# Row gathers begun during the routing stage, query weights' low parts on another engine, packed activations and a deeper ring of weight tiles

## The chip, the cores and the metric

The kernel runs on one core of one Trainium2 chip. The metric is the device time of one execution in microseconds, the median of three runs. Engines are named as in the profile: PE is TensorE, PEld its weight loads, DVE is VectorE, ACT is ScalarE, POOL is GpSimd, SP is SyncE, which here only issues DMAs.

## The reference, cut to what matters

One layer of a streaming encoder on 512 frames of width 2048: two token mixers (an RWKV7 recurrence and a sparse attention), a residual sum, then a PEER feed-forward block and a last RMS norm. The change touches the PEER block alone:

```python
q = (h @ w_query).reshape(B, T, 8, 2, 128)
s = jnp.einsum('bthcq,hcnq->bthcn', q, sub_keys)      # 128 keys a side
s1, i1 = lax.top_k(s[..., 0, :], 16)
s2, i2 = lax.top_k(s[..., 1, :], 16)
cand, cand_id = s1[..., :, None] + s2[..., None, :], i1[..., :, None] * 128 + i2[..., None, :]
top_s, pos = lax.top_k(cand.reshape(..., 256), 16)
eid, gate = take(cand_id, pos), softmax(top_s)
act = gelu(einsum('nd,nhkd->nhk', hx, expert_u[eid]))   # 16384 experts
y = einsum('nhk,nhkd->nd', gate * act, expert_v[eid])
```

Every token has 8 heads x 16 chosen experts, that is 128 rows of `expert_u` and 128 rows of `expert_v`.

## The kernel before

Weights are fp32 in HBM. To multiply them with nearly fp32 precision in the fast fp32r format, each 128x1024 weight tile (`raw`, 512 KB, loaded by SP's queue) is split: ACT copies its rounded high part (`whi`, line 198), DVE subtracts to get the low part (`wlo`, line 199), and PE does three matmuls for each product (high x high, high x low, low x high). `load_w` does this; the pool `wp` holds three `raw`, two `whi` and two `wlo`. `load_w` runs at a raised priority, so that weights are placed ahead of other work.

The order of each engine's queue is not the order of the program: a planner (the tile framework) orders the instructions by priority and by the times of a model, places buffers, and puts in the waits. Each engine then works through its own queue in order. `issue_after(x)` keeps the DVE instructions of a block behind instruction x.

The PEER block splits the tokens. The first 176 tokens are computed by gathering: for each chosen expert a row of 8 KB is fetched for each of 128 partitions by an indirect DMA from POOL (line 1005, 1 MB each, 176 from `ru` and 176 from `rv`), into three buffers (`rows`); DVE makes a dot product (line 1015) or adds a scaled row (line 1023). They come in three groups, of 16 tokens (16 items each way), 32 tokens (32) and 128 tokens (128); with the start and end of each group 364 items in all. The other 336 tokens (`ND`) are computed densely: all 16384 experts on PE, weighted by a matrix G that is zero where an expert was not chosen. This part has the following stages:

- `route`: for 8 heads x 2 sides a gemm of the query weights (512 tokens), scores, and the top-16 search on DVE (`top16`); per head four pieces of "early" dense experts (24 of 128 column groups are computed early, to use PE; their weights come through an own pool `we`). The expert numbers of the 128-token group, `eid[-1]`, are written head by head.
- G, still in `route`: for each token a one-hot product builds the columns of G, with POOL, ACT and DVE making the one-hots (`oa`, `ob`) and PE multiplying; G goes to HBM (`d_g`), and the remaining early pieces run between.
- `experts`: 16 column groups; in each, 8 activations (`act`, 336 columns, 48 matmuls each, lines 214 to 216), `gated` by G (line 1210) and split into `Wh`, `Wl`; then 16 blocks of output features with 24 matmuls each (lines 1229 to 1231), added into `accT` (line 1236). G is loaded for each column group by POOL's queue into one buffer (line 1200). Between, `step` takes up gather items at a fixed rate, each behind the last `wlo` of `load_w`.

The normalized activations of all 512 tokens, split into `h2h` and `h2l`, stay in SBUF (64 KB a partition) until the last activation; their space is then used for the final buffers (`fin`).

Of the kernel before, what the change touches and what calls it, by code (L numbers as in the profile page):

```python
# [167 lines left out]
class Kernel:  # L168
    def __init__(self, tc, io, out, dbg=None):
        self.tc, self.nc, self.io, self.out, self.dbg = tc, tc.nc, io, out, dbg or {}  # L170
        self.fins = ExitStack()
        self.blocks = ((0, 128), (1, 128), (2, ND - 256))
# [16 lines left out]
    def load_w(self, src, wp=None):  # L189

        nc = self.nc
        wp = wp or self.wp
        with self.tc.high_priority(offset=100):
            raw = wp.tile([128, 1024], F32, tag="raw", name="raw", bufs=3)
            nc.sync.dma_start(raw, src.rearrange("p a b -> p (a b)"))
            hi = wp.tile([128, 1024], F32R, tag="whi", name="whi")
            lo = wp.tile([128, 1024], F32R, tag="wlo", name="wlo")
            nc.scalar.activation(hi, raw, AF.Copy)  # L198
            self.last = nc.vector.tensor_tensor(lo, raw, hi.bitcast(F32), op=ALU.subtract).ins  # L199
        return hi, lo  # L200
# [736 lines left out]
    def peer(self):  # L937
# [3 lines left out]
        with ExitStack() as es:  # L941
# [38 lines left out]
            self.hs = lambda k: (hh[:, k, NG:T], hl[:, k, NG:T])  # L980
            with ExitStack() as es2:
                self.route(es2, lambda k: (hh[:, k], hl[:, k]))
            self.dp = R(self.pool("dense", side="right"))
# [4 lines left out]
    def step(self, items, n=1):  # L988

        self.due += n * self.rate  # L990
        while self.due >= 1:
            self.due -= 1
            with self.tc.issue_after(self.last):
                next(items, None)

    def gathered(self):
# [11 lines left out]
        for i, (t0, m, parts) in enumerate(GROUPS):  # L1008
            eid, act, n = self.eid[i], self.act_[i], 128 // parts
# [3 lines left out]
            for s in range(n):  # L1013
                r = rows(io["ru"], eid, s)
                v.tensor_tensor_reduce(r, r, h, 1.0, 0.0, op0=ALU.mult, op1=ALU.add, accum_out=act[:, s:s + 1])  # L1015
                yield
            sc.activation(act, act, AF.Gelu)
            v.tensor_tensor(act, act, self.gate[i], op=ALU.mult)
            o = row("out")
            for s in range(n):  # L1020
                r = rows(io["rv"], eid, s)
# [23 lines left out]
            yield  # L1045

# [10 lines left out]
    def route(self, es, xs):  # L1057
# [12 lines left out]
        with ExitStack() as es3:  # L1070
            tp = es3.enter_context(self.pool("top", 2))
            ts = tp.tile([128, 4, 8, 16], F32, name="ts", bufs=1)
            sel = [tp.tile([128, 4, 8, 16], F32, name=f"sel{i}", bufs=1) for i in range(2)]
            for h in range(8):
                sv = tp.tile([128, 2, 4, 16], F32, name="sv")
                si = tp.tile([128, 2, 4, 16], U32, name="si")
                sf = tp.tile([128, 2, 4, 16], F32, name="sf")
# [45 lines left out]
                for e, b in ((self.eid[-1], 0), (eid1, 1)):  # L1123
                    m = e.shape[0]
                    v.scalar_tensor_tensor(e[:, 16 * h:16 * h + 16], sel[0][:m, b, h], 128.0, sel[1][:m, b, h], op0=ALU.mult, op1=ALU.add)

# [23 lines left out]
        for tg in range(ND // 16):  # L1150
            Gs = gp.tile([128, 128, 16], F32, name="Gs")
            for b in range(4):
                i = 4 * tg + b
                n = 4 * len(EARLY) - 32
                for _ in range((i + 1) * n // (ND // 4) - i * n // (ND // 4)):
                    next(early, None)
                pg = self.wk()
# [31 lines left out]
    def experts(self):  # L1189
# [3 lines left out]
        items = self.gathered()  # L1193
        self.due = 0
        self.rate = sum(2 * (128 // g[2]) + 4 for g in GROUPS) / (256 + 2 * (128 - len(EARLY)) - 20)
        ng = ND // 16
        for cg in range(16):
# [3 lines left out]
            W = []  # L1201
            for j in range(8):
# [6 lines left out]
                a3 = a.rearrange("p (g t) -> p g t", g=ng)  # L1209
                v.tensor_tensor(a3, a3, G[:, :, j], op=ALU.mult)  # L1210
                wh = dp.tile([128, ND], F32R, name="Wh", bufs=8)
                wl = dp.tile([128, ND], F32R, name="Wl", bufs=8)
                self.split(a, wh, wl)
                W.append((wh, wl))
                if e not in EARLY:
                    self.step(items, 2)
            turn = iter(())
            if last:
                for _ in items:
                    pass  # L1220
                self.left.close()
                turn = self.turned()
            for db in range(16):
# [14 lines left out]
                self.step(items)  # L1238
# [4 lines left out]
    def turned(self):  # L1243
# [3 lines left out]
        self.fp = self.fins.enter_context(self.pool("fin"))  # L1247
# [52 lines left out]
```

## Time and profile before

| | |
|---|---|
| runs, us | 4098.62, 4097.76, 4099.79; median 4098.62 |
| profiled execution, us | 4096.14 |
| its span, us | 4094.4 |
| mean granted clock of PE | 0.985 |
| busy share PE, DVE, ACT, POOL | 95%, 70%, 34%, 23% |
| DMA moved | 946 MB, 231 GB/s over the span |

The span is what the trace covers; the execution's own time is 1.7 us longer. Matmuls overlap in the array, so PE can be busy without being at its peak; counts of matmuls in a stretch tell more than its busy share. A wait is put down to the releaser that came last.

### The profile page before, as it was taken

What the parts mean: (1) busy time and instruction counts of PE and PEld (TensorE: products, weight loads), DVE (VectorE), ACT (ScalarE), POOL (GpSimd) and SP (SyncE); (2) the same over time, 40 slices, a digit from 0 to 9 for tenths busy, and PEclk for the clock granted to TensorE, in tenths of its full rate; (3) what the DMA queues carried; (4) which work ended last, traced back from release to release, by engine and by line L of the source; (5) the groups of instructions that cost most, each with busy time, mean ns of one, the idle gap of its engine ahead of it and who ended that gap; (6) DMA issues with size and microseconds to landing.
All of it is one profiled execution on the core that took longest, in us unless ns stands there. A gap on an engine that the chain in (4) does not pass through costs nothing. (4 is left out here: it accounts for less than half of the span.)

```text
span 4094.4 us, 57543 instructions
## 1 busy us (share of the span) xinstructions
PE 3903.1 (95%) x22241; PEld 3511.4 (86%) x22241; DVE 2861.5 (70%) x4766; ACT 1393.1 (34%) x2044; POOL 958.7 (23%) x980
## 2 busy tenths in 40 slices
PE   8999999999998999999998999999999999999998
PEld 6777778888886788788898899999999999899998
DVE  5445588444434552489876778889888888889885
ACT  4222332222224422332486333333333233333333
POOL 2101210101104300100363323323332233333220
PEclk9999999999999999999999999999999999999999
DMA  4333842332327433443576989989999999999994
GB/s 150 125 125 132 198 165 83 103 101 84 99 86 199 143 131 137 144 134 107 185 220 184 346 309 368 373 310 367 360 368 369 361 370 353 353 363 367 348 352 168
DMA packets 258290, 946.17 MB, mean 231 GB/s; under 512 B 28224, under 2 KB 77504, under 8 KB 209280
## 3 DMA queue, kind: packets, MB, share of 16 engines
q1 hardware_dynamic: 132528, 445.76, 31.9%
q0 software_dynamic: 82144, 474.71, 31.3%
q10 hardware_dynamic: 43344, 22.02, 1.9%
q8 instruction: 175, 2.87, 0.3%
q14 instruction: 99, 0.81, 0.1%
HBM read 866.18 MB, written 76.12 MB: 230 GB/s over the span
## 5 line engine op out<-in xcount | busy, mean ns | idle before, releaser
L198 ACT ACTIVATE whi<-raw 128x1024 fp32r<-128x1024 f32 x758 | 802.8, 1060 | 1953.6 <-PE mm L215 871.1
L199 DVE TENSOR_TENSOR wlo<-raw,whi 128x1024 fp32r<-128x1024 f32 x758 | 927.2, 1225 | 708.3 <-ACT whi L198 645.5
L1231 PE MATMUL wk<-Wh,wlo 128*128 128x336 f32 x2048 | 658.6, 323 | 57.2 <-DVE wlo L199 57.0
L1229 PE MATMUL wk<-Wh,whi 128*128 128x336 f32 x2048 | 660.4, 323 | 16.1 <-ACT whi L198 10.9
L1230 PE MATMUL wk<-Wl,whi 128*128 128x336 f32 x2048 | 657.1, 321 | 2.3 <-DVE Wl L228 2.2
L214 PE MATMUL mm<-h2h,whi 128*128 128x336 f32 (+1 forms) x1920 | 630.6, 328 | 12.8 <-ACT gel L1181 10.9
L216 PE MATMUL mm<-h2h,wlo 128*128 128x336 f32 (+1 forms) x1920 | 630.8, 329 | 8.5 <-DVE wlo L199 8.2
L215 PE MATMUL mm<-h2l,whi 128*128 128x336 f32 (+1 forms) x1920 | 629.6, 328 | 0.0
L214 PE MATMUL mm<-xh,whi 128*128 128x512 f32 x1168 | 473.3, 405 | 2.1 <-ACT xh L346 1.5
L216 PE MATMUL mm<-xh,wlo 128*128 128x512 f32 x1168 | 468.2, 401 | 6.0 <-DVE wlo L199 6.0
L215 PE MATMUL mm<-xl,whi 128*128 128x512 f32 x1168 | 470.2, 403 | 0.6 <-POOL xl L348 0.5
L1231 PEld LDWEIGHTS wk<-Wh,wlo 128*128 128x128 f32 x2048 | 391.4, 191 | 73.5 <-DVE wlo L199 71.3
L1015 DVE CUSTOM_DVE_ANT_0 rows<-rows,h2t 128x2048 f32<-128x2048 f32 x176 | 401.7, 2284 | 44.6 <-DMA rows<-in_ru_dram,eid 44.4
L1023 DVE SCALAR_TENSOR_TENSOR out<-rows,act,out 128x2048 f32<-128x2048 f32 x173 | 405.7, 2345 | 20.8 <-DMA rows<-in_rv_dram,eid 20.0
L1229 PEld LDWEIGHTS wk<-Wh,whi 128*128 128x128 f32 x2048 | 392.2, 192 | 26.2 <-ACT whi L198 16.8
L1005 POOL DMA_INDIRECT rows<-in_ru_dram,eid x176 | 263.9, 1500 | 595.2 <-DVE act L1015 540.7
L1005 POOL DMA_INDIRECT rows<-in_rv_dram,eid x176 | 258.8, 1470 | 600.1 <-DVE out L1023 531.2
L1230 PEld LDWEIGHTS wk<-Wl,whi 128*128 128x128 f32 x2048 | 392.1, 191 | 4.3 <-DVE Wl L228 3.9
L216 PEld LDWEIGHTS mm<-h2h,wlo 128*128 128x128 f32 x1920 | 363.6, 189 | 25.6 <-DVE wlo L199 15.1
L214 PEld LDWEIGHTS mm<-h2h,whi 128*128 128x128 f32 x1920 | 363.6, 189 | 24.1 <-ACT gel L1181 11.4
L215 PEld LDWEIGHTS mm<-h2l,whi 128*128 128x128 f32 x1920 | 363.7, 189 | 10.0 <-issue 0.2
L216 PEld LDWEIGHTS mm<-xh,wlo 128*128 128x128 f32 x1168 | 221.6, 190 | 60.3 <-DVE wlo L199 6.9
(432 smaller groups left out, 5711.4 us busy)
## 6 DMA issues: line engine op xcount, KB each, us to landing
raw<-in_pu_dram SPq DMA_DIRECT2D x256, 512.0 KB
raw<-in_pv_dram SPq DMA_DIRECT2D x256, 512.0 KB
raw<-in_w_in_dram SPq DMA_DIRECT2D x146, 512.0 KB
d_g<-Gs ACTq DMA_DIRECT2D x21, 1024.0 KB
G<-d_g POOLq DMA_DIRECT2D x16, 1344.0 KB
raw<-in_wbr_dram SPq DMA_DIRECT2D x32, 512.0 KB
raw<-in_wout_dram SPq DMA_DIRECT2D x32, 512.0 KB
raw<-in_wpq_dram SPq DMA_DIRECT2D x32, 512.0 KB
```

Of the source, the lines that this page charges most:

```text
L198: nc.scalar.activation(hi, raw, AF.Copy)
L199: self.last = nc.vector.tensor_tensor(lo, raw, hi.bitcast(F32), op=ALU.subtract).ins
L214: nc.tensor.matmul(ps, hi[:, s], xh, start=k == 0, stop=False)
L215: nc.tensor.matmul(ps, hi[:, s], xl, start=False, stop=False)
L216: nc.tensor.matmul(ps, lo[:, s], xh, start=False, stop=k == nk - 1)
L1005: nc.gpsimd.indirect_dma_start(out=r, out_offset=None, in_=table, in_offset=bass.IndirectOffsetOnAxis(ap=eid[:, s:s + 1], axis=0))
L1015: v.tensor_tensor_reduce(r, r, h, 1.0, 0.0, op0=ALU.mult, op1=ALU.add, accum_out=act[:, s:s + 1])
L1023: v.scalar_tensor_tensor(o, r, act[:, s:s + 1], o, op0=ALU.mult, op1=ALU.add)
L1229: mmul(ps, hi[:, s], wh, start=j == 0, stop=False)
L1230: mmul(ps, hi[:, s], wl, start=False, stop=False)
L1231: mmul(ps, lo[:, s], wh, start=False, stop=j == 7)
```

## The change

Gather items begin in the route: two after each head, and one after every sixth of the 84 steps of G, 30 in all. For this the 128-token group's dot products come first, then the two small groups whole, then the rest of the 128-token group. During the heads, the low parts of the query weights are subtracted on POOL and not on DVE (those of early experts stay on DVE). The index tile `sf` is bf16 in place of fp32. At the end of the route, ACT and DVE copy the 336 dense tokens of `h2h` and `h2l` into packed tiles (43 KB a partition), and the old 64 KB are freed; the dense buffers and a new pool `wx` go there. `wx` has two `raw`, one `whi` and one `wlo`, which `load_w` uses in turn with those of `wp` in the dense stage, by the counter `nw`. In the first column group the six experts that are not early come first, and gating lags two experts behind. The final buffers use the packed tiles' space.

```diff
@@ load_w
+        pr = ps = wp
+        if self.wx and wp is self.wp:
+            pr, ps = wp if self.nw % 5 < 3 else self.wx, wp if self.nw % 3 < 2 else self.wx
+            self.nw += 1
-            raw = wp.tile([128, 1024], F32, tag="raw", name="raw", bufs=3)
+            raw = pr.tile([128, 1024], F32, tag="raw", name="raw", bufs=3 if pr is wp else 2)
-            hi = wp.tile([128, 1024], F32R, tag="whi", name="whi")
-            lo = wp.tile([128, 1024], F32R, tag="wlo", name="wlo")
+            hi = ps.tile([128, 1024], F32R, tag="whi", name="whi")
+            lo = ps.tile([128, 1024], F32R, tag="wlo", name="wlo")
-            self.last = nc.vector.tensor_tensor(lo, raw, hi.bitcast(F32), op=ALU.subtract).ins
+            if self.low is nc.vector or wp is not self.wp:
+                self.last = nc.vector.tensor_tensor(lo, raw, hi.bitcast(F32), op=ALU.subtract).ins
+            else:
+                self.low.tensor_tensor(lo, raw, hi.bitcast(F32), op=ALU.subtract)
@@ peer
+            self.items, self.nitems = self.gathered(), 0
             with ExitStack() as es2:
                 self.route(es2, lambda k: (hh[:, k], hl[:, k]))
-            self.dp = R(self.pool("dense", side="right"))
+            self.packed = ExitStack()
+            hp = self.packed.enter_context(self.pool("h2d", side="right"))
+            ph = hp.tile([128, 16, ND], F32R, name="ph")
+            pl = hp.tile([128, 16, ND], F32R, name="pl")
+            for a, b in ((0, 2), (2, 6), (6, 11), (11, 16)):
+                sc.activation(ph[:, a:b], hh[:, a:b, NG:T], AF.Copy)
+                v.tensor_copy(pl[:, a:b], hl[:, a:b, NG:T])
+            self.left.close()
+            self.hs = lambda k: (ph[:, k], pl[:, k])
+            self.wx = E(self.pool("wx", 1))
+            self.dp = E(self.pool("dense"))
@@ step
+    def item(self):
+        self.nitems += 1
+        with self.tc.issue_after(self.last):
+            next(self.items, None)
@@ gathered: up(i) and down(i) are the two halves of the old loop over groups
+        last = len(GROUPS) - 1
+        yield from up(last)
+        for i in range(last):
+            yield from up(i)
+            yield from down(i)
+        yield from down(last)
@@ route
+            self.low = nc.gpsimd
             for h in range(8):
-                sf = tp.tile([128, 2, 4, 16], F32, name="sf")
+                sf = tp.tile([128, 2, 4, 16], BF16, name="sf")
...
+                for _ in range(2):
+                    self.item()
+            self.low = v
...
+                if i % 6 == 5:
+                    self.item()
@@ experts
-        self.rate = sum(2 * (128 // g[2]) + 4 for g in GROUPS) / (256 + 2 * (128 - len(EARLY)) - 20)
+        self.rate = (sum(2 * (128 // g[2]) + 4 for g in GROUPS) - self.nitems) / (256 + 2 * (128 - len(EARLY)) - 20)
+            js = list(range(8))
+            if first:
+                js = [j for j in js if 8 * cg + j not in EARLY] + [j for j in js if 8 * cg + j in EARLY]
+            for j in js:
...
+                wait.append((j, a))
+                while len(wait) > (2 if first else 0):
+                    gated(*wait.pop(0))
                 if e not in EARLY:
-                    self.step(items, 2)
+                    self.step(2)
+            for w in wait:
+                gated(*w)
...
-                self.left.close()
+                self.packed.close()
@@ turned
-        self.fp = self.fins.enter_context(self.pool("fin"))
+        self.fp = self.fins.enter_context(self.pool("fin", side="right"))
```

## Rows read from the trace of the kernel before

**Rows 1.** Table of stretches: us, then busy us and instructions of each engine, granted clock, DMA share, GB/s.

```profile
1735.00:1998.00 263.00, 258.70 (x1324) 223.00 (x1322) 236.63 (x963) 79.14 (x97) 16.71 (x32) 0.99 0.38 125
1998.00:2215.00 217.00, 205.20 (x1470) 198.95 (x1470) 166.62 (x470) 163.99 (x302) 142.13 (x189) 1.00 0.70 217
2215.00:2240.00 25.00, 14.39 (x66) 14.11 (x67) 9.39 (x15) 6.17 (x11) 2.53 (x2) 0.74 0.52 153
2240.00:4012.00 1772.00, 1687.42 (x10613) 1652.07 (x10613) 1512.94 (x1481) 567.40 (x689) 540.08 (x373) 0.98 0.94 353
```

**Rows 2.** Who TensorE waited for, 2240 to 4012: us in total, times, longest.

```profile
PE wk L1231 <- DVE wlo L199: 56.5, 41, 6.2
```

**Rows 3.** Who ScalarE waited for, 2240 to 4012.

```profile
ACT whi L198 <- DMA raw<-in_pv_dram: 220.3, 71, 8.4
...
ACT whi L198 <- DMA raw<-in_pu_dram: 148.5, 58, 4.4
```

**Rows 4.** Who VectorE waited for, 2240 to 4012.

```profile
DVE rows L1015 <- DMA rows<-in_ru_dram,eid: 44.4, 28, 6.3
...
DVE out L1023 <- DMA rows<-in_rv_dram,eid: 20.0, 21, 2.9
```

**Rows 5.** Instructions in order of time around one stall; in brackets the wait before.

```profile
3783.37 1.45 POOL L1200 DMA_DIRECT2D G<-d_g  x1
...
3791.09 0.31 PE L1231 MATMUL wk<-Wh,wlo 128*128 128x336 f32 x1
...
3791.55 0.31 PE L1231 MATMUL wk<-Wh,wlo 128*128 128x336 f32 x1
...
3794.88 1.06 ACT L198 ACTIVATE whi<-raw 128x1024 fp32r<-128x1024 f32 x1 [6.36 <-DMA raw<-in_pv_dram]
...
3797.46 0.51 DVE L1210 TENSOR_TENSOR gel<-gel,G 128x336 f32<-128x336 f32 x1 [4.99 <-DMA G<-d_g]
...
3801.84 0.65 PE L1231 MATMUL wk<-Wh,wlo 128*128 128x336 f32 x1 [5.27 <-DVE wlo L199]
```

**Rows 6.** Table of windows of 20 us around that stall; columns as in the first group.

```profile
3740.00:3760.00 20.00, 20.00 (x132) 20.00 (x132) 18.65 (x17) 7.86 (x12) 7.71 (x5) 1.00 0.93 346
...
3780.00:3800.00 20.00, 15.09 (x88) 13.05 (x86) 13.82 (x13) 4.77 (x6) 5.06 (x4) 1.00 1.02 387
3800.00:3820.00 20.00, 18.16 (x102) 18.16 (x103) 17.35 (x15) 4.24 (x4) 5.53 (x4) 0.83 0.82 311
```

**Rows 7.** Groups by line, POOL, 1998 to 2215: count, busy us, mean ns, idle before.

```profile
L1005 POOL DMA_INDIRECT rows<-in_ru_dram,eid x7 | 10.1, 1448 | 17.5 <-DVE oa L1168 9.7 <-DVE act L1015 4.3 <-DMA eid<-eid 2.8
```

**Rows 8.** Groups by line, VectorE, 1998 to 2215.

```profile
L1015 DVE CUSTOM_DVE_ANT_0 rows<-rows,h2t 128x2048 f32<-128x2048 f32 x4 | 9.1, 2278 | 0.0
```

**Rows 9.** TensorE in order of time, 2216 to 2240: the matmuls that waited.

```profile
2216.70 0.63 PE L214 MATMUL mm<-h2h,whi 128*128 128x336 f32 x1 [2.01 <-ACT gel L1181]
...
2234.80 0.65 PE L214 MATMUL mm<-h2h,whi 128*128 128x336 f32 x1 [8.91 <-ACT gel L1181]
```

**Rows 10.** POOL in order of time, 2215 to 2240.

```profile
2221.75 1.52 POOL L1200 DMA_DIRECT2D G<-d_g  x1 [16.27 <-DMA d_g<-Gs]
```

**Rows 11.** The tile gel: duration ns lowest/median/highest, first and last start.

```profile
L1210 DVE TENSOR_TENSOR gel<-gel,G x128: 487/500/509, 2231.5 to 4013.5; 128x336 f32<-128x336 f32 x128
...
L1181 ACT ACTIVATE gel<-mm x104: 425/431/451, 2216.2 to 4012.2; 128x336 f32<-128x336 f32 x104
```

**Rows 12.** Groups by line, VectorE, 1735 to 1998.

```profile
L199 DVE TENSOR_TENSOR wlo<-raw,whi 128x1024 fp32r<-128x1024 f32 x51 | 61.8, 1214 | 15.5 <-ACT whi L198 15.5
...
L1119 DVE TENSOR_TENSOR oh<-oh,sf 128x1024 bf16<-128x1024 bf16 x15 | 18.2, 1216 | 0.0
```

**Rows 13.** Instructions in order of time, 29 to 33: subtracts of 512 columns.

```profile
28.73 0.68 DVE L348 TENSOR_TENSOR xl<-xT,xh 128x512 fp32r<-128x512 f32 x1
...
28.90 1.65 POOL L348 TENSOR_TENSOR xl<-xT,xh 128x512 fp32r<-128x512 f32 x1 [20.10 <-ACT xh L346]
...
29.99 1.11 DVE L348 TENSOR_TENSOR xl<-xT,xh 128x512 fp32r<-128x512 f32 x1
```

More of the change, by code (lines that the diff above doesn't have):

```diff
@@ L171, in __init__ @@
         self.fins = ExitStack()
+        self.wx, self.nw, self.low = None, 0, self.nc.vector
         self.blocks = ((0, 128), (1, 128), (2, ND - 256))
@@ L986, in peer, with step @@
             self.right.close()
-    def step(self, items, n=1):
+    def step(self, n=1):
         self.due += n * self.rate
@@ L992, in step @@
             self.due -= 1
-            with self.tc.issue_after(self.last):
-                next(items, None)
+            self.item()
[3 more added lines that the diff above has]
+            next(self.items, None)
     def gathered(self):
@@ L1007, in rows, with up @@
             return r
-        for i, (t0, m, parts) in enumerate(GROUPS):
-            eid, act, n = self.eid[i], self.act_[i], 128 // parts
+        def up(i):
+            t0, m, parts = GROUPS[i]
             h = row("h2t")
@@ L1012, in gathered, with down @@
                 nc.gpsimd.dma_start(h[m * j:m * j + m], self.d_h2[t0:t0 + m])
-            for s in range(n):
-                r = rows(io["ru"], eid, s)
-                v.tensor_tensor_reduce(r, r, h, 1.0, 0.0, op0=ALU.mult, op1=ALU.add, accum_out=act[:, s:s + 1])
+            for s in range(128 // parts):
+                r = rows(io["ru"], self.eid[i], s)
+                v.tensor_tensor_reduce(r, r, h, 1.0, 0.0, op0=ALU.mult, op1=ALU.add, accum_out=self.act_[i][:, s:s + 1])
                 yield
+        def down(i):
+            t0, m, parts = GROUPS[i]
+            act = self.act_[i]
             sc.activation(act, act, AF.Gelu)
@@ L1019, in gathered @@
             o = row("out")
-            for s in range(n):
-                r = rows(io["rv"], eid, s)
+            for s in range(128 // parts):
+                r = rows(io["rv"], self.eid[i], s)
                 if s:
@@ L1156, in route @@
                     next(early, None)
+                if i % 6 == 5:
+                    self.item()
                 pg = self.wk()
@@ L1192, in experts @@
         dp = self.dp
-        items = self.gathered()
         self.due = 0
-        self.rate = sum(2 * (128 // g[2]) + 4 for g in GROUPS) / (256 + 2 * (128 - len(EARLY)) - 20)
+        self.rate = (sum(2 * (128 // g[2]) + 4 for g in GROUPS) - self.nitems) / (256 + 2 * (128 - len(EARLY)) - 20)
         ng = ND // 16
@@ L1200, in experts, with gated @@
             nc.gpsimd.dma_start(G.rearrange("p g e t -> p g (e t)"), self.d_g[:, cg].rearrange("g p f -> p g f"))
-            W = []
-            for j in range(8):
+            W, wait = {}, []
+            def gated(j, a):
+                a3 = a.rearrange("p (g t) -> p g t", g=ng)
+                v.tensor_tensor(a3, a3, G[:, :, j], op=ALU.mult)
+                wh = dp.tile([128, ND], F32R, name="Wh", bufs=8)
+                wl = dp.tile([128, ND], F32R, name="Wl", bufs=8)
+                self.split(a, wh, wl)
+                W[j] = wh, wl
+            js = list(range(8))
+            if first:
+                js = [j for j in js if 8 * cg + j not in EARLY] + [j for j in js if 8 * cg + j in EARLY]
+            for j in js:
                 e = 8 * cg + j
@@ L1208, in experts @@
                     a = run(self.act(e, self.mm()))
[L1209 to L1214, printed above, removed]
+                wait.append((j, a))
+                while len(wait) > (2 if first else 0):
+                    gated(*wait.pop(0))
                 if e not in EARLY:
-                    self.step(items, 2)
+                    self.step(2)
+            for w in wait:
+                gated(*w)
             turn = iter(())
             if last:
-                for _ in items:
+                for _ in self.items:
                     pass
-                self.left.close()
+                self.packed.close()
                 turn = self.turned()
@@ L1237, in experts @@
                 next(turn, None)
-                self.step(items)
+                self.step()
         for _ in turn:
```

## Prediction

> **What bounds the kernel now.** I read the table of stretches first [rows 1]. It cuts the part of the span that the diff touches: the route (263 us up to 1998), the building of G (to 2215), a join of 25 us, and the dense stage with the row gathers beside it (2240 to 4012). In the dense stage TensorE is busy 1687 of 1772 us, VectorE 1513, and the DMA engines 0.94 of the time at 353 GB/s: three resources near their ends. The next question is what a TensorE that never waits would need. In an undisturbed stretch every third matmul starts 0.46 us after the one before of its kind [rows 5], so one takes 0.153 us; the 10613 of the dense stage [rows 1] are 1629 us. So 143 of 1772 us are lost. Idle time gives 85 of them; the mean granted clock is 0.98 (of 2.4 GHz; after a wait matmuls run at the lower level, 1.2), some 28 us more; 30 us I cannot name. By far the most waited for is the low part of a weight: line 1231, on VectorE's subtract of line 199, 56.5 us in 41 waits [rows 2].
>
> Why is the low part late? ScalarE's copy of the high part waits 369 us for weights to land (220.3 + 148.5) [rows 3], and VectorE 64 us for gathered rows (44.4 + 20.0) [rows 4]. One stall in order of time shows the links [rows 5]: at 3783.4 the load of the next G is issued among the gathers and weights; the next weight tile is copied only at 3794.9, after a wait of 6.36 us; VectorE stands 4.99 us before a product with G, and with it the subtract queued behind; TensorE then stands 5.27 us. The windows around it [rows 6] show the cost: 132 matmul records in an undisturbed 20 us, 88 and 102 in the two with the stall, the second at a granted clock of 0.83. A weight tile lasts 24 matmuls, 3.7 us, and the kernel has three raw tiles and two split pairs. So the dense stage is held by weights that come late out of a full DMA, with little in store.
>
> **The change part by part.**
>
> *Gathers moved forward.* 30 items (16 in the route, 14 in G) run before the dense stage. Already now 7 gathers [rows 7] and 4 dot products [rows 8] are taken up in G, so 23 gathers and 26 dot products leave the dense stage. A gather is 128 x 2048 fp32, 1.05 MB: 24 MB, at 353 GB/s [rows 1] 68 us of DMA. The dot products are 26 x 2.28 = 59 us of VectorE [rows 8], out of 1513.
>
> *More weight tiles.* Five raw tiles for three and three split pairs for two: one more pair is 3.7 us more of work in store, two more raw tiles give a load 7.4 us more of lead. The shown stall of 5.27 us would shrink by 3.7, to 30%.
>
> *Dense stage, sum.* If only bytes count, it gains 68 us; if every loss shrinks as the shown stall would, 0.70 x 143 = 100. I take the middle, 85; the ends are 21 (the second rival) and 143.
>
> *Join.* Packing copies 16 slices: on ScalarE 16 x 0.43 = 6.9 us, on VectorE at most 16 x 0.50 = 8 us beside it [rows 11]. The packed tiles are opened where the route's and G's pools were just closed, so I take it that they wait for the last stores of G; the load of G, which waits for the same stores, starts at 2221.75 [rows 10]. Two slices later, at about 2222.7, TensorE can begin. It now begins at 2216.70 but stands again for 8.91 us [rows 9], because gel tiles are held until G has landed. Between 2215 and 2240 only 66 records run [rows 1] where 163 would fit: 15 us lost. After: 8 us idle, 2 at the low clock, 1 for the first of the new tiles, which cannot load before the packing has read the old ones: 11. The edit that starts the other six experts first and delays gating by two keeps TensorE running meanwhile. Join: -4 us, ends -10 and +8. Loads for the new tiles wait on SP's queue; behind them stand later weights and the stored activations.
>
> *G stage.* 14 gathers and dot products for 7 and 4: POOL gets 7 x 1.45 = 10 us on 142 of 217, VectorE 10 x 2.28 = 23 us on 167 [rows 1, 7, 8]. Both have room, and TensorE, busy 205, is the bound. At worst VectorE's 23 us come on top; at best nothing. I take 6, since VectorE is 77% busy and work that falls between is mostly hidden.
>
> *Route.* VectorE is busy 237 of 263 us, TensorE 259 [rows 1]. The 32 subtracts of query weights leave VectorE: -32 x 1.21 = -39 us [rows 12]; the 16 dot products come: +37 us [rows 8]. The bf16 index tile makes 16 multiplies (1.22 us each, 19 us in all [rows 12]) cheaper by an amount between nothing and all; they are nearest to their own row, and I take nothing. On POOL a 128x512 subtract takes 1.65 us [rows 13], so 128x1024 is estimated at 3.3: 106 us for 32; with 16 gathers at 1.45 (23 us) and now 17 us busy about 146 of 263. POOL has the time, but not the freedom. VectorE's subtract that starts beside POOL's takes 1.11 us, the one that starts first 0.68 [rows 13]: they hold each other up. VectorE keeps some 83 instructions with two SBUF inputs in the route (32 for the one-hots, 16 candidate sums, 19 early weights, 16 dot products). If POOL is in a subtract 40% of the time (106 of 263) and such an instruction then waits half a subtract, that is 83 x 0.40 x 1.65 = 55 us: VectorE's demand goes from 237 to 290, over the 263, less what falls into its waits. I take +14 us; the ends are -19 (the multiplies free) and +78 (each subtract holds VectorE for its full length: 237 - 2 + 106 = 341).
>
> The Trainium skill's page SBUF — State Buffer, section "Who interferes with whom", says that VectorE and GpSimd share one pair of ports as an exclusive lock, and that a VectorE instruction with two SBUF inputs contends with a GpSimd instruction that reads SBUF. The trace agrees: the VectorE subtract begun at 29.99 ends at 31.10, half a microsecond after POOL's (28.90 to 30.55) has let go [rows 13]. With the rule pushed to its end the route's term would be the +78 in place of +14.
>
> *Waits added.* A gather on POOL waits for a row buffer and its indices; behind it now stand low parts of query weights and the sub-key loads, and TensorE waits for these. Two split pairs are all that covers this.
>
> *Order of groups, the tail.* The same items run in another order, 30 of 364 fewer beside the dense work; the final buffers wait for the packed tiles' last reader instead of the old ones', the same matmul. Nothing.
>
> Sum: -85 - 4 + 6 + 14 = -69 us.
>
> **The rivals.**
> 1. Only the bytes count: deeper stores help nothing because a full DMA delivers at its rate whoever asks. For it: 0.94 share over the stage; against it: full 132 records in a window at 0.93 [rows 6]. Dense -68, in all -52: 4047 us.
> 2. Trade: weights now ask for more at once, gathers land later, VectorE stands before them. Its 64 us of waits for rows [rows 4] double; dense -21, in all -5: 4094, no change. Against it: gathers have three buffers and some 5 us between them.
> 3. Slower: POOL's queue in the route. Each of 16 gathers waits for a row buffer that a dot product behind the top-16 search frees, and the low parts wait behind it. The longest such wait in G was 9.7 us [rows 7]: 16 x 9.7 = 155 in place of the 14, in all +72: 4171. The seven gathers of G waited 17.5 us together [rows 7], 2.5 each, and at that it would be 40 and still a gain. The sign turns at 83/16 = 5.2 us each.
> 4. The ports are a full lock: route +78, in all -5: 4094. Against it: not every VectorE instruction has two SBUF inputs (the searches have one).
> 5. The change doesn't do it: the planner that orders the queues may place the route's items in G or later. Then only some 7 more gathers move: bytes -21, deeper stores -17, join -4, in all -42: 4057.
>
> **How the numbers follow.** The profiled execution is 4096.1 us, 1.7 over its span; the median of the runs is 2.5 above it. 4096.1 - 69 + 2.5 = 4030. Chances: forecast 0.58, rival one 0.17, two 0.05, three 0.09, four 0.05, five 0.06. A measurement of this kernel tells about 0.2%, 8 us, from no change. Faster: forecast, one and five, and the better part of four's milder forms, 0.83; same: two and the rest of four, 0.08; slower: three, 0.09. The range: dense -115 with the other terms at nothing gives 3985; above it goes to 4085, which takes in one and five and leaves out two, three and four. The forecast's own range is 3985 to 4065.
>
> **What would show it.** Right: dot products before 2000; POOL subtracts near 3.3 us in the route; waits of the low-part matmul in the dense stage under half of 56.5 us; waits for weights well under 369 us; 353 GB/s or more over a dense stage of about 1690 us. Wrong: a route well over 263 us with TensorE waiting for POOL (rival three) or with VectorE's two-input instructions stretched (four); VectorE's waits for rows over 100 us (two); gathers first issued after 2000 (five); TensorE standing long after 2215 because packing waits for more than G's stores.

## The result and the profile after

The changed kernel takes 4038.24 us (median of four runs, 4035.43 to 4038.96) beside 4098.19 us for the kernel before (four runs, 4097.5 to 4099.79): a ratio of 0.9852, with a 95% interval from 0.9835 to 0.9869. It is faster by 60 us; 4030 was predicted, in a range from 3985 to 4085.

The spans of the two profiled executions, 4094.4 and 4036.9, differ by 57.5 us. To say where, I cut both at the same five instructions, by their start times: ScalarE's first copy of h2h (the route begins), the first one-hot `ob` (G begins), the last copy of G's columns `Gs` (the join begins), the first matmul of the expert-down product (the dense stage proper), the last gelu (the tail). Every length in this table is a difference of two such times in one profiled execution; the time is the median of the kernel's runs.

| us | time | route | G | join | dense | tail |
|---|---|---|---|---|---|---|
| before | 4098 | 291.5 | 203.9 | 44.9 | 1752.6 | 82.2 |
| after | 4038 | 319.5 | 202.4 | 66.2 | 1649.7 | 81.4 |
| difference | | +28.0 | -1.5 | +21.3 | -102.9 | -0.8 |

With a route that begins 1.6 us earlier these add up to the 57.5. So the dense stage gave 103 us, and the route and the join took almost half of it back. TensorE's matmuls moved too: the route has 21 fewer of them than before, G 75 fewer, the join 96 more, and the dense stage the same 10487. At the prediction's 0.1535 us for a matmul (1629 us for 10613) those 96 are 15 of the join's 21 us.

The table of stretches of the kernel after, cut where [rows 1] cut the one before (columns as there):

```profile
1733.00:2024.00 291.00, 265.39 (x1326) 227.25 (x1325) 263.21 (x968) 77.93 (x96) 134.65 (x88) 0.97 0.56 190
2024.00:2241.00 217.00, 195.73 (x1376) 187.83 (x1374) 183.50 (x485) 163.27 (x299) 150.81 (x196) 0.98 0.77 242
2241.00:2266.00 25.00, 19.42 (x118) 19.42 (x119) 14.04 (x12) 10.85 (x11) 4.95 (x3) 0.86 0.67 213
2266.00:3955.00 1689.00, 1657.82 (x10656) 1648.48 (x10656) 1459.15 (x1438) 572.37 (x697) 519.23 (x343) 0.99 0.93 354
```

The route's work takes 291 us where it took 263, with TensorE busy 265 in place of 259: it waits now. The dense stretch holds 43 more matmuls than before in 83 us less, at the same rate of the DMA (354 GB/s, 353 before). At 0.1535 us, 10656 of them are 1636 us, so 53 us are lost where 143 were.

Who TensorE waited for in the dense stretch of the kernel after, and two rows of VectorE's waits (total, times, longest):

```profile
PE wk L1283 <- ACT Wh L236: 23.2, 5, 13.3
PE wk L1284 <- DVE Wl L237: 6.6, 5, 2.2
PE mm L225 <- DVE wlo L206: 1.3, 1, 1.3
...
DVE out L1052 <- DMA rows<-in_rv_dram,eid: 36.6, 21, 4.5
...
DVE rows L1040 <- DMA rows<-in_ru_dram,eid: 20.8, 8, 6.5
```

The wait for a weight's low part, 56.5 us in [rows 2], is 1.3. ScalarE's waits for weights to land, 369 us in [rows 3], have no row in this stretch any more: it waits for TensorE to give a split tile back. VectorE's waits for gathered rows, 64 us in [rows 4], are 57: they are still there, but they no longer reach TensorE through the low parts.

Now the route. Its window as cut in the table of stages, then its largest waits and groups (TensorE's waits; VectorE's wait for the scores `S`; groups of VectorE; groups of POOL; 1733 to 2024):

```profile
1717.70:2037.20 319.50, 290.60 (x1464) 248.35 (x1463) 283.28 (x997) 95.09 (x123) 153.84 (x105) 0.97 0.57 199
...
PE mm L225 <- POOL wlo L208: 14.1, 6, 6.9
PE wk L1126 <- DMA sk<-in_subk_dram: 5.3, 1, 5.3
...
DVE sv L1088 <- ACT S L1128: 13.7, 3, 7.2
...
L1040 DVE CUSTOM_DVE_ANT_0 rows<-rows,h2t 128x2048 f32<-128x2048 f32 x17 | 48.4, 2845 | 5.2 <-DMA rows<-in_ru_dram,eid 5.2
L206 DVE TENSOR_TENSOR wlo<-raw,whi 128x1024 fp32r<-128x1024 f32 x22 | 28.6, 1301 | 7.7 <-ACT whi L204 7.7
...
L1152 DVE CAST pf<-u 128x64 f32<-128x64 uint32 x8 | 13.8, 1731 | 0.0
L1157 DVE TENSOR_TENSOR oh<-oh,sf 128x1024 bf16<-128x1024 bf16 x15 | 13.1, 872 | 0.0
...
L208 POOL TENSOR_TENSOR wlo<-raw,whi 128x1024 fp32r<-128x1024 f32 x30 | 73.8, 2467 | 63.5 <-ACT whi L204 63.3
```

POOL's subtract takes 2.47 us (3.3 was estimated). The dot product takes 2.85 us in the mean where it took 2.28 [rows 8], and a cast of 64 numbers 1.73 us; before it took 0.185. The means hide two kinds: 5 of the 17 dot products took 3.75 to 4.42 us and the other 12 stayed at 2.26 to 2.29, and 5 of the 8 casts took 2.62 to 2.68 and the others 0.18 to 0.19. Each of the ten stretched ones ran beside a subtract on POOL, and none of the others did. Two places in order of time show why (VectorE and POOL, each pair side by side):

```profile
1856.26 2.62 DVE L1152 CAST pf<-u 128x64 f32<-128x64 uint32 x1
...
1856.46 2.36 POOL L208 TENSOR_TENSOR wlo<-raw,whi 128x1024 fp32r<-128x1024 f32 x1
...
1881.38 2.40 POOL L208 TENSOR_TENSOR wlo<-raw,whi 128x1024 fp32r<-128x1024 f32 x1 [11.08 <-ACT whi L204]
...
1881.50 4.42 DVE L1040 CUSTOM_DVE_ANT_0 rows<-rows,h2t 128x2048 f32<-128x2048 f32 x1
```

The subtract of 1881.38 ends at 1883.78; the dot product issued 0.12 us behind it ends at 1885.92, 2.14 us after that, which is about its own length: it stood through the whole subtract. The cast ends at 1858.88, the subtract beside it at 1858.82.

And the join, in order of time (ScalarE, VectorE, TensorE, SP's queue):

```profile
2245.76 4.97 ACT L999 ACTIVATE ph<-h2h 128x672 fp32r<-128x672 f32 x4 [5.19 <-DMA d_g<-Gs]
...
2245.88 4.90 DVE L1000 CAST pl<-h2l 128x672 fp32r<-128x672 f32 x4 [11.77 <-DMA d_g<-Gs]
...
2246.58 0.65 PE L223 MATMUL mm<-ph,whi 128*128 128x336 f32 x1 [7.07 <-ACT ph L999]
...
2294.11 0.95 SPq L1261 DMA_DIRECT2D gel<-d_a  x2
...
2304.69 0.51 DVE L1248 TENSOR_TENSOR gel<-gel,G 128x336 f32<-128x336 f32 x1 [4.17 <-DMA gel<-d_a]
...
2305.76 0.65 PE L1283 MATMUL wk<-Wh,whi 128*128 128x336 f32 x1 [13.30 <-ACT Wh L236]
2308.59 0.65 PE L1284 MATMUL wk<-Wl,whi 128*128 128x336 f32 x1 [2.18 <-DVE Wl L237]
```

Packing waits for G's last store, as predicted, and TensorE for packing, 7.07 us. But then TensorE stands 13.30 us before the first expert-down matmul: that one needs the first expert of the group, an early one, whose stored activations are gated last and are asked for only at 2294.11.

### The profile page after: what moved, and what is told of

Same layout as the page of the kernel before. It is cut to its first block, busy times and chain, and to the rows that moved or that the text cites. A ratio compares the mean times of both kernels' runs of the same rounds, so it can differ in the third digit from the quotient of the medians.

```text
span 4036.9 us, 57519 instructions
## 1 busy us (share of the span) xinstructions
PE 3876.1 (96%) x22241; PEld 3506.1 (87%) x22241; DVE 2851.8 (71%) x4738; ACT 1399.3 (35%) x2048; POOL 1069.1 (26%) x1012
## 4 chain that ended last, share of the span: by engine, by line
PE 53%; DVE 5%; DMA 5%; issue 2%; POOL 2%; ACT 1%; DVEq 0%; SPq 0%; ACTq 0%; POOLq 0%
PE wk L1283 8%; PE wk L1284 8%; PE wk L1285 8%; PE mm L225 7%; PE mm L224 7%; PE mm L223 7%; DMA rows<-in_rv_dram,eid 2%; PE wk L870 1%; PE wk L869 1%; PE wk L868 1%; DVE wlo L206 1%; PE wk L1213 1%; DMA rows<-in_ru_dram,eid 1%; DVE rows L1040 1%; POOL rows L1030 1%
## 5 line engine op out<-in xcount | busy, mean ns | idle before, releaser
L206 DVE TENSOR_TENSOR wlo<-raw,whi 128x1024 fp32r<-128x1024 f32 x726 | 889.0, 1225 | 644.3 <-ACT whi L204 581.6
L1285 PE MATMUL wk<-Wh,wlo 128*128 128x336 f32 x2048 | 649.7, 318 | 0.0
L223 PE MATMUL mm<-ph,whi 128*128 128x336 f32 x1664 | 526.7, 317 | 7.1 <-ACT ph L999 7.1
L225 PE MATMUL mm<-ph,wlo 128*128 128x336 f32 x1664 | 527.3, 317 | 1.3 <-DVE wlo L206 1.3
L224 PE MATMUL mm<-pl,whi 128*128 128x336 f32 x1664 | 526.5, 316 | 0.0
L1030 POOL DMA_INDIRECT rows<-in_rv_dram,eid x176 | 277.9, 1579 | 592.6 <-DVE out L1052 488.2
L1030 POOL DMA_INDIRECT rows<-in_ru_dram,eid x176 | 274.2, 1558 | 604.5 <-DVE act L1040 487.7
L223 PEld LDWEIGHTS mm<-ph,whi 128*128 128x128 f32 x1664 | 313.3, 188 | 7.7 <-ACT ph L999 7.3
L225 PEld LDWEIGHTS mm<-ph,wlo 128*128 128x128 f32 x1664 | 312.7, 188 | 1.7 <-DVE wlo L206 1.6
L224 PEld LDWEIGHTS mm<-pl,whi 128*128 128x128 f32 x1664 | 313.7, 189 | 0.5 <-issue 0.5
```

The source lines that it names most:

```text
L223: nc.tensor.matmul(ps, hi[:, s], xh, start=k == 0, stop=False)
L224: nc.tensor.matmul(ps, hi[:, s], xl, start=False, stop=False)
L225: nc.tensor.matmul(ps, lo[:, s], xh, start=False, stop=k == nk - 1)
L1285: mmul(ps, lo[:, s], wh, start=False, stop=j == 7)
```

## The experiments

Each kernel is the one after with the edit shown. In the expectations on the dense stage, theory A says that moved bytes bring most of the gain and the deeper store of weights the rest, B that the store does nearly all, C that only bytes count. Stage lengths are cut as above, in one profiled execution each; that of e8 took 10 us more than the median of its runs and that of e11 6 us more, so their lengths lean high.

| us | time (runs) | ratio to before, 95% | route | G | join | dense |
|---|---|---|---|---|---|---|
| e1_no_ring | 4117.64 (4) | 1.0035, 1.0015 to 1.0055 | 317.9 | 201.9 | 65.1 | 1730.4 |
| e2_ring_only | 4025.93 (2) | 0.9820, 0.9791 to 0.9848 | 293.1 | 192.0 | 64.4 | 1677.9 |
| e7_raw_only | 4120.33 (8) | 1.0051, 1.0038 to 1.0065 | 317.4 | 202.2 | 64.5 | 1733.2 |
| e8_pair_only | 4081.08 (7) | 0.9948, 0.9933 to 0.9964 | 321.3 | 203.0 | 69.6 | 1696.4 |
| e11_no_ring_two_g | 4137.01 (2) | 1.0090, 1.0058 to 1.0122 | 318.8 | 202.5 | 70.8 | 1746.4 |
| e3_low_dve | 4025.69 (2) | 0.9819, 0.9791 to 0.9848 | 306.6 | 204.7 | 63.9 | 1649.8 |
| e6_act_cast | 4052.55 (2) | 0.9881, 0.9858 to 0.9903 | 330.8 | 204.3 | 66.6 | 1649.5 |
| e4_first_pv_order | 4029.66 (2) | 0.9829, 0.9800 to 0.9857 | 316.9 | 201.9 | 52.9 | 1654.0 |
| e5_ring_join | 4026.19 (4) | 0.9819, 0.9801 to 0.9837 | 291.6 | 202.2 | 39.1 | 1688.8 |
| e9_low_dve_join | 4022.25 (4) | 0.9807, 0.9786 to 0.9829 | 306.5 | 219.6 | 41.9 | 1655.7 |
| e10_g_items_join | 4009.54 (4) | 0.9778, 0.9754 to 0.9802 | 293.1 | 217.0 | 40.6 | 1658.1 |
| e12_g_items_order | 4009.05 (4) | 0.9782, 0.9765 to 0.9798 | 293.6 | 204.8 | 52.9 | 1654.3 |

### Which half of the change brings the gain

e1 leaves the new tiles out, e2 the moved gathers (with the low parts back on VectorE and the index tile in fp32).

```diff
# e1_no_ring
-            self.wx = E(self.pool("wx", 1))
# e2_ring_only
-            self.low = nc.gpsimd
-                sf = tp.tile([128, 2, 4, 16], BF16, name="sf")
+                sf = tp.tile([128, 2, 4, 16], F32, name="sf")
-                for _ in range(2):
-                    self.item()
-                if i % 6 == 5:
-                    self.item()
```

> The changed kernel (4038 us) without the two extra raw tiles and the extra split pair; all else stays. Theory A (moved bytes and deeper ring share the gain, as the prediction had it: 68 of 85 us by bytes): the dense stage from the first expert-down matmul to the last activation matmul takes 1648 + about 25 us, the run about 4065, and waits of the low-part matmul come back to some 20 us. Theory B (the ring does nearly all, moved gathers little): 1648 + 80 or more, the run about 4120, low-part waits back near 56 us. Theory C (only bytes count): no difference, about 4038.

> The changed kernel with the deeper ring and the packing but no gather moved forward, all low parts on VectorE and the index tile fp32, so that route and G do the work of the kernel before. The route should go back to 263 us (-26). Theory A: the dense stage loses the 68 us that the bytes were worth: 4038 - 26 + 68 = 4080. Theory B: it loses at most 25: 4037 or less, and moving gathers was not worth its price in the route. Theory C: 4038 - 26 + 85 = 4097.

Dense stage: 1752.6 before, 1730.4 with the moved gathers alone (-22), 1677.9 with the tiles alone (-75), 1649.7 with both (-103). Without the tiles the change is slower than no change at all. Its dense window, the wait of TensorE that matters, and VectorE's largest waits for a transfer:

```profile
2302.50:4032.90 1730.40, 1664.05 (x10487) 1637.21 (x10488) 1429.89 (x1402) 562.11 (x679) 461.77 (x337) 0.98 0.91 338
...
PE wk L1284 <- DVE wlo L206: 46.5, 31, 4.9
...
DVE gel L1247 <- DMA G<-d_g: 30.8, 7, 6.3
DVE rows L1039 <- DMA rows<-in_ru_dram,eid: 14.6, 5, 5.0
DVE out L1051 <- DMA rows<-in_rv_dram,eid: 11.1, 6, 5.2
```

With 31 gathers fewer in the stage (133 and 176 issued, 164 and 176 before) the DMA's share falls to 0.91 and its rate to 338 GB/s, and TensorE still waits 46.5 us for low parts. Without the tiles a gather moved out is worth 22/31 = 0.7 us, not the 2.97 that its bytes take at 353 GB/s. The window with the tiles alone, and the same waits:

```profile
2263.10:3941.00 1677.90, 1642.03 (x10487) 1628.09 (x10488) 1485.80 (x1458) 556.98 (x679) 576.89 (x365) 0.99 0.96 366
...
PE wk L1280 <- DVE wlo L206: 4.6, 8, 1.9
...
DVE out L1052 <- DMA rows<-in_rv_dram,eid: 53.4, 29, 5.5
...
DVE rows L1040 <- DMA rows<-in_ru_dram,eid: 42.6, 27, 6.1
```

VectorE's waits for rows are now 96 us, more than the 64 of [rows 4], and TensorE's wait for low parts is 4.6. The stops are as many; with the tiles they hardly reach TensorE through the low parts. Theory B holds, with its bound for e2 just passed: the dense stage loses 28 us without the moved gathers, where it allowed 25. As a whole e2 is even 12 us faster than after, so the moved gathers with their low parts did not pay for their place; the two intervals overlap a little.

### Which tiles: raw tiles, split pairs, or the stops themselves

e7 keeps the two raw tiles alone, e8 the third pair alone. e11 has no new tiles but a second buffer for G, so that VectorE need not stand before it.

```diff
-            pr, ps = wp if self.nw % 5 < 3 else self.wx, wp if self.nw % 3 < 2 else self.wx
# e7_raw_only
+            pr = wp if self.nw % 5 < 3 else self.wx
# e8_pair_only
+            ps = wp if self.nw % 3 < 2 else self.wx
# e11_no_ring_two_g (e1, and)
-            G = dp.tile([128, ng, 8, 16], F32, name="G")
+            G = dp.tile([128, ng, 8, 16], F32, name="G", bufs=2)
```

> The changed kernel with the two extra raw tiles but only two split pairs. If lead for the loads is what the ring gives (ScalarE waited 369 us for weights, which the ring took away), the main dense stage takes 1650 to 1670 us and the run is under 4060. If ready pairs are what it gives, it stays near the 1730 us of the kernel without the ring: about 4115.

> The changed kernel with the extra split pair but three raw tiles. If lead for the loads is what counts, the main dense stage takes some 1710 us or more and the run is about 4100; if ready pairs count, about 1670 and 4060.

> e1_no_ring (4118 us: gathers moved forward, three raw tiles, two split pairs) with two buffers for G in place of one. If the stalls without the ring come from VectorE standing before a product with G (31 us in 7 waits there), those waits go and the main dense stage falls from 1730 to about 1690 us, the run to about 4078. If they come from anything that stops VectorE's queue now and then (rows, stored activations), it falls by less than 15 us.

e7, the largest waits of TensorE and of ScalarE in the dense stage:

```profile
PE wk L1285 <- DVE wlo L206: 57.0, 26, 6.1
...
ACT whi L204 <- PE wk L1284: 666.8, 234, 10.2
ACT whi L204 <- PE mm L224: 330.5, 193, 2.7
```

ScalarE never waits for a weight to land, and nothing is gained: 57 us of TensorE's waits, 1733 us. So the waits of [rows 3] were not what TensorE's stalls came from. e8 is the reverse:

```profile
ACT whi L204 <- DMA raw<-in_pv_dram: 350.4, 130, 6.7
...
ACT whi L204 <- DMA raw<-in_pu_dram: 168.7, 84, 4.6
...
PE wk L1283 <- ACT Wh L236: 46.9, 15, 14.8
...
PE mm L225 <- DVE wlo L206: 2.7, 5, 1.2
PE wk L1285 <- DVE wlo L206: 2.0, 3, 1.0
```

519 us of ScalarE's waits for weights, more than before, but only 2.7 + 2.0 us of TensorE's for low parts (in the up and the down products), and 34 us gained over e1. TensorE now waits for the gated weights `Wh`, which ScalarE also makes, in the queue in which it waits for raw tiles. Over e1 the raw tiles give +3, the pair -34, both -81; the rows suggest that each takes away what would hold up the other. e11 took away VectorE's waits for G, but it now stood before the stored activations, and the dense stage was 16 us longer than e1's where the expectation had it 40 shorter, or less than 15:

```profile
DVE gel L1247 <- DMA gel<-d_a: 45.9, 19, 5.0
```

Why the stops moved there and cost more was not settled.

### The route: the shared lock or the moved items

e3 puts the low parts back on VectorE, and keeps all 30 items early. e6 leaves them on POOL, and moves the cast that is held up to ScalarE.

```diff
# e3_low_dve
-            self.low = nc.gpsimd
# e6_act_cast
-                v.tensor_copy(pf[1], u[0])
+                sc.activation(pf[1], u[0], AF.Copy)
```

> The changed kernel with the low parts of the query weights on VectorE again; the gathers stay in the route. Theory A (the route is bound by VectorE's work, which POOL's subtracts stretch): VectorE takes 29 to 32 subtracts of 1.21 us back (+37) and loses the stretching of the dot products, casts and low parts beside POOL (-24): route 291 + 13 = 304 us, the run about 4050. Rival (TensorE's waits for POOL, 14 us, and the clock after them lengthen the route): route back towards 270, the run about 4018.

> The changed kernel (4038 us) with the one small cast of the route that was stretched from 0.19 to 1.73 us (8 times, 13.8 us) moved from VectorE to ScalarE. Theory (VectorE's time sets the route): the route falls by about 12 us, the run to about 4026. Rival (POOL simply holds the next two-input instruction of VectorE in its place, or the route is set by TensorE's waits): under 4 us.

e3's route is 13 us shorter than that of after, and the whole 12.6 us faster. Its groups on VectorE (1733 to 2010):

```profile
L206 DVE TENSOR_TENSOR wlo<-raw,whi 128x1024 fp32r<-128x1024 f32 x52 | 62.6, 1205 | 10.7 <-ACT whi L204 10.7
L1040 DVE CUSTOM_DVE_ANT_0 rows<-rows,h2t 128x2048 f32<-128x2048 f32 x17 | 38.6, 2269 | 1.3 <-issue 0.6 <-DMA rows<-in_ru_dram,eid 0.6
...
L1156 DVE TENSOR_TENSOR oh<-oh,sf 128x1024 bf16<-128x1024 bf16 x15 | 10.0, 670 | 0.0
...
L1151 DVE CAST pf<-u 128x64 f32<-128x64 uint32 x8 | 1.7, 209 | 0.0
```

Without subtracts on POOL the dot product takes 2.27 us again, the cast 0.21 and the bf16 multiply 0.67. But VectorE's work is not what made the route of after longer. Its window in e3, beside that of after above:

```profile
1717.50:2024.10 306.60, 286.16 (x1473) 247.16 (x1472) 288.02 (x1028) 95.80 (x123) 70.23 (x75) 0.98 0.61 206
```

VectorE is busy 288 of 306.6 us in e3 and 283 of 319.5 in after: the subtracts that left it (30 x 1.2 = 36 us) and what POOL's subtracts stretched nearly cancel. By the trace of after, 14 of VectorE's instructions in the route were stretched, each beside a subtract: the five dot products, the five casts and four others, 31 us in all. It is idle 36 us in after and 19 in e3. In after it waits 13.7 us for scores, in e3 2.0; TensorE waits 14.1 us there for low parts from POOL and 5.3 for a table of sub-keys, which POOL's queue loads. So the 13 us are waits behind POOL's queue, as far as the rows tell, and that is the rival's side of e3's expectation (its theory had the route 13 us longer); no run takes away the waits and leaves the lock.

The other half of the +28 is the moved items: e3's route is 13.5 us longer than e2's, which has none there (e9 and e10, below, differ by these 16 alone, and by 13.4). e6 was slower by 14 us, against both sides of its expectation. The next two-input instruction took 1.64 us in the mean where after has 1.22; ScalarE stood 29.7 us before its new cast for VectorE's `u`, and TensorE waited for ScalarE:

```profile
L1156 DVE TENSOR_TENSOR oh<-pf,con 128x1024 bf16<-128x1024 f32 x14 | 23.0, 1640 | 0.6
...
PE wk L1126 <- ACT pq L1122: 20.3, 5, 5.9
```

### The join, and the best version

e4 lets the first group's expert-down products run in the order in which the experts are gated, the early ones last. e5 is e2 with that order and with two dense experts computed before packing ("PRE" below), since packing had pushed TensorE's dense matmuls out of G.

```diff
# e4_first_pv_order
-                for j in range(8):
+                for j in js:
# PRE, in e5, e9, e10
+            self.pre = [(j, run(self.act(j, self.mm()))) for j in (2, 3)]
             self.packed = ExitStack()
```

> The changed kernel with one order changed: the matmuls of each expert-down block go over the experts of a column group in the order in which they were gated (in the first group 2 to 7, then 0 and 1), so that the first ones do not begin with the two that were gated last. Theory A (TensorE's wait of 13.3 us at the first of these matmuls is this order's): the wait goes, with 2.2 us behind it and some 3 us of the lower clock: about 4020. Rival (weights and gathers behind it are late anyway, the wait moves on): over 4032.

> The deeper ring without moved gathers (e2_ring_only, 4026 us), with two edits at the join: the first two dense experts are multiplied from the unpacked tiles before the packing, as the kernel before did inside the G stage, and the expert-down matmuls go in the order of gating. Theory (the join is 20 us longer than before because packing shuts these 96 matmuls out of the G stage, and because of the order): the time from the last G copy to the first expert-down matmul falls from 64 to some 40 us, the G stage grows by up to 7, the run about 4007. Rival (the G stage has no room for them and weights wait there): G grows by the 15 us that the matmuls take, the run about 4016.

e4 takes 13.3 us off the join, the length of the wait at 2305.76, and 8.6 off the time. In e5 the join falls by 25 us from e2's, but G grows by 10 and the dense stage by 11, with the DMA at 0.96 and 368 GB/s, and the time is that of e2. Of the 288 matmuls of the first group's six dense experts 96 ran ahead of the join before and none after. From 2005 on, in G, they are 59 records before; e10 gets them back (one of three lines alike in each, before at 2005 to 2215, then e10 at 2011 to 2228):

```profile
L216 PE MATMUL mm<-h2h,wlo 128*128 128x336 f32 x20 | 6.5, 325 | 0.0
```

```profile
L225 PE MATMUL mm<-h2h,wlo 128*128 128x336 f32 x22 | 7.1, 324 | 0.0
```

The last three put together what paid. e9 is e3 with the order of e4 and PRE; e10 is e9 without the items of the route, so that only the 14 of G run early; e12 is e10 without PRE.

> The changed kernel with low parts back on VectorE (e3_low_dve, 4026 us) and the two edits of the join (first two dense experts ahead of the packing, order of the expert-down matmuls). Theory (in e5_ring_join the 25 us won at the join were lost again because, with all gathers in the dense stage, the DMA engines are its bound at 0.96 and 368 GB/s; with gathers moved forward they are at 0.93 and it can be kept): join 64 to about 40 us, G up to 10 longer, dense stage as before at 1650, the run about 4012. Rival (the dense stage is not bound by bytes, the join's gain is lost for another reason): dense stage longer by 10 or more again, the run about 4024.

> As e9_low_dve_join, without the 16 items in the route: only the 14 in G are moved forward. The route goes back by 13 us to 293. If the items are worth in the dense stage about what they cost before it (1 us each), the run is within 4 us of e9_low_dve_join; if the dense stage is bound by bytes (2.97 us a gather), it is 16 x 2.97 - 13 = 34 us slower than that; if they are worth nothing, 13 faster.

> As the run with the items of G alone (4009.5 us, dense 1658, join 41, G 217), but without the two experts of the dense stage that run before packing. If TensorE's work that was pushed out of G behind the packing is worth what the join shows (12 us), this kernel is some 8 to 12 us slower, 4018 to 4022: join 53, G 201 to 205. If the work is only moved from one side of the packing to the other (G took 15 us more for it there), nothing is lost: 4005 to 4012, G 201 to 205, join 53, dense 1650 to 1658.

e10 and e12 take 4009.5 and 4009.1 us, the fastest of all, with intervals that lie clear of that of after. e9 was expected at 4012 and came at 4022: the join fell as hoped (64 to 42), but G grew by 15 us and the dense stage by 6. PRE is worth nothing: what it takes from the join (53 to 41) it adds to G (205 to 217). The items of the route weren't worth their place either. e12's dense window shows it:

```profile
2267.20:3921.50 1654.30, 1631.66 (x10488) 1620.23 (x10488) 1465.62 (x1443) 562.46 (x684) 556.50 (x355) 0.99 0.95 366
```

With 151 and 176 gathers left in it, the stage takes 1654.3 us; e4, which has the same order and 16 gathers fewer there (135 and 176), takes 1654.0. At 0.1535 us a matmul the 10488 are 1610 us: with the tiles the stage is near what TensorE needs, and fewer gathers than these have nothing left to give.

The 14 items of G are another matter. e5 and e10 differ by them alone (and by the type of the index tile, in the route). Their dense windows, e5 first:

```profile
2250.00:3938.80 1688.80, 1648.24 (x10488) 1631.91 (x10488) 1499.44 (x1476) 561.88 (x686) 590.99 (x370) 0.99 0.96 368
```

```profile
2268.70:3926.80 1658.10, 1633.62 (x10489) 1621.12 (x10488) 1468.40 (x1447) 562.61 (x684) 563.30 (x356) 0.99 0.95 366
```

Fourteen gathers out of the stage make it 30.7 us shorter, 2.2 us each, where without the tiles a gather gave 0.7; the next 16 (e9 against e10) make it 2.4 us shorter together. G grows by 14.8 us for them, and the time falls from 4026 to 4010. So with the tiles the gathers do count, up to a point. Whether by their bytes (2.97 us each at 353 GB/s) or by VectorE's work, which falls by 31.0 us, no run separates.

## Why the prediction was right, and where its steps were not

**The total.** The sum was -69 us, the spans gave -57.5 and the medians -60. The forecast was the likeliest case, and it came. Part of that is luck: the route came out 14 us worse than its term, join and dense stage together 7 worse, and G 7.5 better.

**The dense stage.** Predicted -85. The prediction's stage began at 2240, within the join; in a cut like it (2266 in after) it is -83, and from the first expert-down matmul on it is -103. Join and dense stage together were predicted at -89 and measured at -81.6. The size was right and the split was not: alone, the moved gathers gave 22 and the tiles 75. The step that failed is "24 MB, at 353 GB/s 68 us of DMA": it took the DMA's rate as the bound of the stage as it was. e1 has the bytes gone, and the DMA simply ran at 338 GB/s. Only with the tiles does a moved gather bring more: 30.7 us for the first 14, and 2.4 for the next 16. The 85 was the middle of two sums, and that a middle hit is luck.

The reading behind it, "weights that come late out of a full DMA, with little in store", was half right. Little in store: yes (e2, e8). Late out of the DMA: hardly, since in e7 no weight is late and TensorE waits as long. What stood behind the low parts of [rows 2] was VectorE's queue, in which the subtract stands behind an instruction that waits for G or for rows, as the stall of [rows 5] shows. It is the rule and not one case: in the trace before, in some 45 of the 56.5 us VectorE's longest stop just ahead of the late subtract was for rows or for G, in e7 in 52 of 57. That a third pair made ahead of time covers such a stop, and that two more raw tiles keep ScalarE able to make it, fits e7, e8 and after, but is argued from them. That the loss falls to 30% by the pair alone (3.7 of 5.27 us) was near the mark for pair and tiles together: 143 us of loss fell to 40 in the same terms (1649.7 - 1610).

**The route.** Predicted +14 between -19 and +78, measured +28. Gathers did start there (first at 1782, first dot product at 1787.6). The prediction let the dot products that come and the subtracts that leave cancel, and put the +14 on the lock. Measured, the items cost 13.4 us (e9 against e10, which differ by them alone), and the subtracts on POOL, all in all, 13 more (after against e3). The step that failed is "Waits added": it named the waits for low parts and sub-keys behind POOL's queue and put them at nothing, and they are 14.1 and 5.3 us of TensorE's. The lock was priced at 55 us of VectorE's work, 33 instructions of 1.65 us, and took 31: only 14 were stretched, but most of them by nearly a whole subtract. The cast was missed altogether, since its row has one input: five of eight were held, 12 us in all. The bf16 multiplies were taken at no gain and gave 0.34 us each in the mean of after (0.87 for 1.22 [rows 12]), where one that met a subtract took 3.57 us, and 0.55 in e3.

So rival four was there in a milder form: a lock, but not for all of VectorE's work. The Trainium skill's page SBUF — State Buffer, section "Who interferes with whom", has both halves: an instruction with two SBUF inputs contends with a GpSimd instruction that reads SBUF, and a copy or cast can use the shared pair as well, while a reduction on this chip doesn't. The traces agree: 2.85 against 2.27 us for the dot product, 1.73 against 0.21 for the cast, and the reduction of line 1158 at 1.20 us with POOL's subtracts, five of them beside one, and 1.20 without.

**The join.** Predicted -4 between -10 and +8, measured +21.3 up to the first expert-down matmul. That packing waits for G's last stores was right, and TensorE's 7.07 us of idle time were the predicted 8; in the first 25 us, which is what the prediction priced, 118 matmul records run where 66 did. Two things behind them were missed. The sentence that the new order "keeps TensorE running meanwhile" looked at the six experts that go first and not at the expert-down matmul, which starts with the first early expert, now gated last; it stood 13.30 and then 2.18 us (e4 gives 13 us back). And the 96 dense matmuls that ran ahead of the join before, 15 us, now run in it.

**G.** Predicted +6; e2 against after gives 10.4 us for 14 items, e5 against e10 14.8. After against before shows -1.5, with 75 matmuls, 11.5 us, gone from G.

**The rivals.** Rival one (-68, tiles useless) fell with e1 and e2. Rival two: VectorE's waits for rows didn't double (57 us after); in e2 they rose to 96, and the dense stage still gained 75. Rival three came in small: TensorE waited 14.1 us for POOL's low parts in the route (longest 6.9), and the rows put the cost of the subtracts on POOL there. Rival five is out: 44 of the 176 first gathers were issued before the first expert-down matmul, 12 before.

## What to carry to other kernels

A DMA that is busy 0.94 of a stage isn't yet its bound: ask what the waiting engine stands behind in its own in-order queue, and whether a store in front of it covers the longest of such stops. When the store is deep enough, moving work out of the stage pays until the next bound is reached (here 14 gathers), and then no more; what it costs where it goes has to be set against that. Before work goes to GpSimd, list VectorE's instructions beside it that have two SBUF inputs or that copy or cast, price those that will meet a GpSimd instruction at its length, and ask what waits behind the work in GpSimd's own queue. When a stage is reordered, look at the first consumer of what now comes last, and at what had been running in the stage that the new barrier closes.

## What the runs showed of the hardware that was not expected

- A cast of 64 columns from uint32 to fp32 on VectorE took 2.62 us when it was issued 0.2 us ahead of POOL's subtract in the record, 0.21 without POOL's subtracts (mean of 8).
- POOL's fp32 subtract of 128x1024 took 2.47 us where VectorE's takes 1.21: less than twice the 1.65 us of 128x512 [rows 13].
- The multiply of two bf16 tiles takes 0.67 us, the same with an index tile in fp32 1.22 [rows 12].
- The DMA's rate over the dense stage followed the demand: with all its gathers 354 GB/s at a share of 0.94 before and 366 to 368 at 0.96 with the deeper store (e2, e5); with 31 fewer 338 at 0.91 without it (e1) and 353 at 0.93 with it (after).
